# Trunk of one RG-LRU and one sparse-attention layer on one core: compressed-key scores as columns of the other score products, contiguous first loads

## The chip, the cores and the metric

The kernel runs on one core of one Trainium2 chip. Its time is device microseconds of one execution; three runs of the kernel before give a median of 574.55 us (574.05 to 574.77). The engines are named as in the profile: PE multiplies matrices (PEld loads its stationary operand), DVE and ACT work on rows of 128 partitions, POOL fills small tiles, SP issues most of the transfers. A "step" below is the distance from the start of one instruction to the start of the next on the same engine.

## The reference, cut to what matters

Two layers on x of 256 tokens by 1024 columns. Layer 0 is a recurrent block (two projections, a width-4 convolution, gates, a scan, an output projection), layer 1 is attention with three branches; a squared-ReLU MLP of 4096 follows each, with RMSNorm ahead of each part. The attention branches have their own keys and values and share the queries. With 256 tokens the selected and the window branch see all earlier keys. The compressed branch has 15 keys a group (padded to 16 in the kernel), and the change is about its scores:

```python
s_c = jnp.einsum('qghd,ngd->ghqn', qf, kc) - slopes * d_c.astype(jnp.float32)
p_c = _masked_softmax(s_c, d_c >= 0)
o_c = jnp.einsum('ghqn,ngd->qghd', p_c, vc)
...
s_s = jnp.einsum('qghd,gqkd->ghqk', qf, k_sel) - slopes * d_s[:, None].astype(jnp.float32)
...
s_w = jnp.einsum('qghd,kgd->ghqk', qf, kw) - slopes * d_w.astype(jnp.float32)
```

There are 16 heads in 4 groups of 4, 64 columns a head. Each score is the product of a query with a key, less a slope times the distance; a masked softmax follows for each branch.

## The kernel before

Activations lie transposed (128 columns of the model on the partitions, 256 tokens along the row). Every float32 product with weights is made of three products of float32r halves: a weight piece of 128 x 1024 lands in one of 5 raw buffers (`raw`, NRAW), ACT or DVE copies its high part to `whi` (L316, L268), DVE subtracts to get the low part `wlo` (L313, L277), and PE runs `mm3` (L308 to L310) for each of the 8 blocks of 128. A piece is 24 matmuls of 256 columns. There are 7 places for split pieces.

The two mixer layers are not written in program order: each step is given to a `Plan` with an engine, a cost, the keys that it reads and writes and a due time, and the plan (list scheduling, then passes backwards and forwards, with a seed) decides the order on each engine. HI tasks may go to ACT or DVE. The two MLPs are written out by hand.

**Start.** SP loads x in four parts of two chunks (L523 through `first_load`) and the first three weight pieces in halves (`raw0` keys), in the order of FIRST; the norm's gain for x comes as `vec[:, :8]`, a transfer of 32 bytes a partition that ACT issues (L532). `hh` is x times the gain on ACT (L558), `hl` the rest on DVE (L560). PE first runs WARM = 16 matmuls on a zero tile (L552), which feed nothing, then the first three pieces (the `c0`, `c1`, `c2` projections, in step with the chunks of x as they come).

**Gates.** In the recurrent layer, the square of the decay (`a2`) is a DVE multiplication, four of 128 x 512.

**Attention.** kh and kl hold the high and low part of the selected and the window keys, 512 columns a group; one half of the partitions of `sa` / `sb` holds the high part of a head's query and the other the low part, so that two matmuls (L1089 on kh, L1090 on kl) make the scores. For each head (`scores`) there are two such pairs: the first 128 queries against 2 x 128 keys, the other 128 queries against 2 x 256 keys. Each product goes to one of three PSUM banks in turn, and DVE adds the distances, writes the row and its extreme in one operation (L1096, a custom instruction and a read of its accumulator); ACT takes exponentials (L1099), DVE or ACT rescale (L1118, L1119), PE transposes (L1129) and multiplies with the values (L1144, `pv`). Between these the plan puts projections of queries and of the output as fillers. The compressed scores come from `compressed(a, ...)`, once for each four heads: eight matmuls of 32 columns (L1033; 16 high and 16 low columns of `kc`), then on DVE two additions from PSUM (L1043, L1044), a maximum (L1045), a subtraction (L1046), a product with the slopes (L1048), an exponential on ACT, a mask (L1050), a sum (L1051), the gate and the reciprocal (L1052, L1054), a product (L1055), then a transpose on PE (L1067) and a copy to `pc`, which `pv` reads first.

Of the kernel before, what the change touches and what calls it, by code (L numbers as in the profile page):

```python
# [19 lines left out]
P = 128  # L20
# [20 lines left out]
FIRST = "x0+ 00+ 10+ x2+ 20+ x4+ 02+ 12+ x6+ 22+ piece vec cst piece"  # L41
LAGS = (0.2, 0.25, 0.15, 0.13)

V_GM, V_GF, V_GL = 0, 16, 32
V_CW, V_CB, V_BA, V_BX, V_LAM = 40, 72, 80, 88, 96
V_PEK, V_PEV, V_BG = 104, 120, 136
V_N = 184
C_ID, C_D0, C_D1, C_DC, C_MC, C_BM, C_QS, C_SL = 0, 128, 256, 512, 544, 576, 584, 592
C_N = 608
# [170 lines left out]
def trunk_kernel(ctx: ExitStack, tc: tile.TileContext, x_in, vec_in, const_in, w2_in, wts, out):  # L220
# [40 lines left out]
    def split_hi(eng=None):  # L261
# [6 lines left out]
        (act.copy if eng is None else eng.tensor_copy)(hi_t[i % NSPL][:, :n], raw_t[i % NRAW][:, :n])  # L268
        state["split"] += 1

    def split_lo(eng=None):
# [5 lines left out]
        (eng or dve).tensor_tensor(lo[:, :n], raw_t[i % NRAW][:, :n], hi[:, :n].bitcast(F32), op=OP.subtract)  # L277
# [45 lines left out]
    class Section:  # L323


        def __init__(self):
# [3 lines left out]
            self.seen, self.join = dict(state), 1  # L330
            self.zs = {}

        def load(self, i, t):
            while self.seen["dma"] <= min(i, len(order) - 1):
                j = self.seen["dma"]
                self.seen["dma"] += 1
                self.add("sp", 1.5, lambda e, j=j: load(j), w=[("raw", j % NRAW), "loads"], t=t - 20 + j * 1e-3, lag=2.0)

        def split(self, i, t, lead):
# [3 lines left out]
            hi, lo, rw = hi_t[i % NSPL], lo_t[i % NSPL], raw_t[i % NRAW]  # L343
            if i >= self.seen["split"]:
                self.add([("act", 0.95, 0.0), ("dve", 0.63, HPEN)], copy(hi[:, :n], rw[:, :n]), r=[("raw", i % NRAW)],
                         w=[("hi", i % NSPL)], t=t)
                self.seen["split"] = i + 1
            if i >= self.seen["lo"]:
                self.add("dve", 1.14, diff(lo[:, :n], rw[:, :n], hi[:, :n]),
                         r=[("raw", i % NRAW), ("hi", i % NSPL)], w=[("lo", i % NSPL)], t=t)  # L350
# [104 lines left out]
    xt = xpool.tile([P, KC, S], F32, name="xt")  # L455
# [3 lines left out]
    consts.tile([P, 64], F32, name="edge")  # L459
# [53 lines left out]
    with ExitStack() as ph:  # L513
        rg = ph.enter_context(tc.tile_pool(name="rg", bufs=1))
        sec = Section()
        add, table = sec.add, sec.table
# [5 lines left out]
        def first_load(q, o, i, key, d):  # L522
            add(q, d, lambda e: (nc.scalar if e is act else nc.sync).dma_start(o, i), w=key + ["loads"] * (q == "sp"), t=-29.0, lag=1.9)  # L523

        def first_x(k, n=2):
            first_load("sp", xt[:, k:k + n], x_in[:, k:k + n], [("xt", k + i) for i in range(n)], (0.47, 0.73)[n - 1])

        def first_w(i, q, n=2):
            w = wts[offs[i]:offs[i + 1]].rearrange("(p n) -> p n", p=P)[:, q * 256:(q + n) * 256]
            first_load("sp", raw_t[i][:, q * 256:(q + n) * 256], w, [("raw0", i, q + j) for j in range(n)], (0.47, 0.73)[n - 1])  # L530
        sec.plan.busy["pool"] = 0.9
        nc.scalar.dma_start(vec[:, :8], vec_in[:, :8])  # L532
        add("sp", 0.0, lambda e: None, w=["vec0"], t=-31, lag=2.2)
        sec.seen.update(dma=NFINE, split=NFINE, lo=NFINE)
        for x in FIRST.split():
            n = 1 + x.endswith("+")
            if x == "piece":
                sec.load(sec.seen["dma"], -6)
            elif x == "cst":
                first_load("sp", cst, const_in, ["cst"], 1.0)  # L540
            elif x == "vec":
                first_load("sp", vec[:, 8:], vec_in[:, 8:], ["vec"], 0.47)
            elif x[0] == "x":
                first_x(int(x[1]), n)
            else:
                first_w(int(x[0]), int(x[1]), n)
# [4 lines left out]
        for i in range(WARM):  # L551
            pe.matmul(wz, warm[:, :P], warm, start=True, stop=True)  # L552

        x2 = rg.tile([P, KC, S], F32, name="x2")
        for k in range(KC):
            g = vec[:, V_GM + k:V_GM + k + 1]
# [24 lines left out]
        nc.gpsimd.dma_start(w2raw, w2_in)  # L581
# [797 lines left out]
```

## Time and profile before

| | us |
|---|---|
| median of three runs | 574.55 |
| the profiled execution, its own time | 573.78 |
| span of the profiled execution, first to last instruction | 572.0 |
| PE busy, DVE busy, ACT busy | 562.4, 410.3, 339.5 |
| recurrent layer on PE, about | 6 to 94 |
| first MLP on PE, about | 94 to 270 |
| attention layer on PE, about | 270 to 396 |
| second MLP and end, about | 396 to 572 |

The page gives busy time for each engine; a matmul is counted busy from its start to a modelled end, and matmuls overlap, so that a busy PE says only that it had no long gap. Whether PE lost time is read from the steps between the starts of its matmuls: where work flows, a 256-column matmul starts every 0.113 us, while each is shown as 0.28 us long.

### The profile page before, as it was taken

To read this page: it belongs to the slowest core of one execution; us is meant where nothing else is said; L and a number is where in the kernel's file an instruction comes from. 1 tells how busy PE (TensorE), PEld (TensorE's weight loads), DVE (VectorE), ACT (ScalarE), POOL (GpSimd) and SP (SyncE) were. 2 spreads that over 40 slices of the span, in tenths; PEclk is the share of its full clock that TensorE was granted. 3 is DMA by queue.
4 is the path that set the end of the run, shared out by engine and by line. 5 is a ranking of instruction groups with operands and counts; after the bars stand their busy time and mean duration, and the time that the engine had idled before them with its cause. 6 is when DMAs were issued, how large, how long until landed. Compare 5 with 4: busy or idle time off the path is not lost.

```text
span 572.0 us, 12346 instructions
## 1 busy us (share of the span) xinstructions
PE 562.4 (98%) x4896; PEld 553.3 (97%) x4896; DVE 410.3 (72%) x832; ACT 339.5 (59%) x663; POOL 44.9 (8%) x57
## 2 busy tenths in 40 slices
PE   7999999999999999999999999999999999999995
PEld 7999999999999999999999999899999999999995
DVE  6999999776775564565849999989866775563532
ACT  7699585866564443444557988866865564443410
POOL 2210000000000211221000000000000000222310
PEclk9999999999999999999999999999999999999998
DMA  8934576665667456556685132343676666467302
GB/s 290 395 122 148 171 241 197 211 208 189 190 197 241 150 196 223 170 190 227 213 268 170 35 111 64 141 148 111 215 228 186 190 200 237 150 201 223 129 1 73
DMA packets 32745, 103.66 MB, mean 181 GB/s; under 512 B 4000, under 2 KB 7584, under 8 KB 32688
## 3 DMA queue, kind: packets, MB, share of 16 engines
q1 hardware_dynamic: 31968, 102.36, 55.2%
q8 instruction: 38, 0.62, 0.5%
q10 hardware_dynamic: 688, 0.46, 0.2%
q14 instruction: 19, 0.16, 0.1%
q0 software_dynamic: 32, 0.07, 0.0%
HBM read 99.23 MB, written 1.05 MB: 175 GB/s over the span
## 4 chain that ended last, share of the span: by engine, by line
PE 97%; DVE 1%; DMA 1%; ACT 0%; issue 0%; DVEq 0%
PE bank L310 28%; PE bank L308 28%; PE bank L309 28%; PE bank L1144 3%; PE bank L667 2%; PE bank L1129 2%; PE bank L1089 1%; PE bank L1090 1%; PE bank L981 1%; DMA vec<-in_dram 1%; PE bank L982 1%; PE bank L983 1%; PE bank L931 1%; PE bank L1033 1%; DVE xg L1264 0%; DVE wlo L313 0%
## 5 line engine op out<-in xcount | busy, mean ns | idle before, releaser
L308 PE MATMUL bank<-hhl,whi 128*128 128x256 f32 x768 | 213.4, 278 | 1.3 <-DVE whi L316 1.3
L310 PE MATMUL bank<-hhl,wlo 128*128 128x256 f32 x768 | 212.5, 277 | 0.6 <-DVE wlo L313 0.6
L309 PE MATMUL bank<-hhl,whi 128*128 128x256 f32 x768 | 212.3, 276 | 0.0
L308 PEld LDWEIGHTS bank<-hhl,whi 128*128 128x128 f32 x768 | 144.2, 188 | 1.8 <-ACT whi L316 1.5
L310 PEld LDWEIGHTS bank<-hhl,wlo 128*128 128x128 f32 x768 | 144.2, 188 | 1.0 <-DVE wlo L313 1.0
L277 DVE TENSOR_TENSOR wlo<-raw,whi 128x1024 fp32r<-128x1024 f32 x115 | 143.2, 1266 | 1.9 <-ACT whi L268 1.9
L309 PEld LDWEIGHTS bank<-hhl,whi 128*128 128x128 f32 x768 | 144.2, 188 | 0.2
L308 PE MATMUL bank<-uhl,whi 128*128 128x256 f32 x512 | 141.5, 276 | 0.0
L309 PE MATMUL bank<-uhl,whi 128*128 128x256 f32 x512 | 141.4, 276 | 0.0
L310 PE MATMUL bank<-uhl,wlo 128*128 128x256 f32 x512 | 141.4, 276 | 0.0
L268 ACT CAST whi<-raw 128x1024 fp32r<-128x1024 f32 x116 | 118.1, 1039 | 23.1 <-issue 18.8
L308 PEld LDWEIGHTS bank<-uhl,whi 128*128 128x128 f32 x512 | 96.1, 188 | 0.0
L310 PEld LDWEIGHTS bank<-uhl,wlo 128*128 128x128 f32 x512 | 96.1, 188 | 0.0
L309 PEld LDWEIGHTS bank<-uhl,whi 128*128 128x128 f32 x512 | 96.1, 188 | 0.0
L313 DVE TENSOR_TENSOR wlo<-raw,whi 128x1024 fp32r<-128x1024 f32 (+2 forms) x74 | 79.2, 1093 | 7.8 <-ACT whi L316 7.7
L316 ACT CAST whi<-raw 128x1024 fp32r<-128x1024 f32 (+2 forms) x64 | 61.3, 966 | 18.8 <-DMA raw<-in_dram 5.3
L510 DVE TENSOR_TENSOR xt<-xt,bank 128x256 f32<-128x256 f32 x39 | 15.7, 418 | 74.3 <-PE bank L310 74.2
L764 ACT ACTIVATE u<-t 128x256 f32<-128x256 f32 x64 | 26.7, 417 | 58.1 <-DVE t L759 58.1
L759 DVE SCALAR_TENSOR_TENSOR t<-bank,rstd 128x256 f32<-128x256 f32 x64 | 26.9, 423 | 39.6 <-PE bank L310 39.6
L1099 ACT ACTIVATE pt<-pt,mx 128x128 f32<-128x128 f32 (+1 forms) x64 | 28.6, 450 | 2.9 <-DVE mx L1096 2.7
L480 POOL TENSOR_TENSOR acc<-xt 128x256 f32<-128x256 f32 x2 | 2.9, 1466 | 341.3 <-DVE xt L510 186.7
L766 DVE TENSOR_TENSOR uhl<-u,uhl 128x256 fp32r<-128x256 f32 x64 | 26.7, 416 | 3.0 <-ACT uhl L765 3.0
(207 smaller groups left out, 725.8 us busy)
## 6 DMA issues: line engine op xcount, KB each, us to landing
raw<-in_dram SPq DMA_DIRECT2D x173, 512.0 KB, 4.3
raw<-in_dram SPq DMA_DIRECT2D x4, 560.0 KB, 4.3
gw<-in_dram SPq DMA_DIRECT2D x4, 512.0 KB, 8.1
raw<-in_dram SPq DMA_DIRECT2D x6, 256.0 KB, 5.1
xt<-in_dram SPq DMA_DIRECT2D x4, 256.0 KB, 5.0
pT<-in_dram SPq DMA_DIRECT2D x2, 512.0 KB, 5.9
kh<-kh SPq DMA_DIRECT2D x8, 64.0 KB, 3.2
kl<-tl SPq DMA_DIRECT2D x8, 64.0 KB, 2.9
```

The lines of the kernel that those rows point to most:

```text
L268: (act.copy if eng is None else eng.tensor_copy)(hi_t[i % NSPL][:, :n], raw_t[i % NRAW][:, :n])
L277: (eng or dve).tensor_tensor(lo[:, :n], raw_t[i % NRAW][:, :n], hi[:, :n].bitcast(F32), op=OP.subtract)
L308: pe.matmul(ps, wh, xh, start=start, stop=False)
L309: pe.matmul(ps, wh, xl, start=False, stop=False)
L310: pe.matmul(ps, wl, xh, start=False, stop=stop)
L313: return lambda e: e.tensor_tensor(o, a, h.bitcast(F32), op=OP.subtract)
L316: return lambda e: (e.copy if e is act else e.tensor_copy)(o, a)
L759: dve.scalar_tensor_tensor(t, z, 0.0, rs, op0=OP.max, op1=OP.mult)
L764: act.activation(u, t, AF.Square)
L766: later(lambda: dve.tensor_tensor(ul[m], u, uh[m].bitcast(F32), op=OP.subtract))
L1099: add("act", (0.39, 0.49)[qc], lambda e, row=row, j=j: e.activation(row, row, AF.Exp, bias=mx[:, j:j + 1], scale=-1.0, accum_out=sm[:, j:j ...
L1144: two = lambda c, w, y, **k: [e.matmul(o()[own_(hf), c0 + c.start:c0 + c.stop], w(hf), y(hf), **k) for hf in range(2)]
```

## The change

- The compressed keys move into kh and kl: a group has now 528 columns (first 128 selected keys, 16 compressed keys, the other 128 selected keys, 256 window keys). `kc`, its clearing on POOL and the eight 32-column matmuls of `compressed` are gone.
- A head's scores are three pairs instead of two: 288 columns for the first 128 queries (128 selected + 16 compressed, 128 window + 16 that nobody reads), 272 for the other queries' selected and compressed keys, 256 for their window keys. Each pair takes one of the same three banks.
- For each head, two DVE operations of 128 x 16 with the accumulator (L1116 of the new kernel) take the compressed scores out of the banks, with distance and slope; `compressed` keeps its steps from the subtraction on, without the slopes' product. Its due times move from 0.5, 4, 8.5, 12 to 3.5, 7.5, 11.5, 15.2 (in units of a head's 5 us), after the heads that feed it.
- x, the gain and the halves of the first three pieces lie in DRAM so that each first transfer reads one contiguous block; the gain comes as 8 more columns of the first x transfer (520 columns) and ACT's transfer is gone. The constants are 592 columns instead of 608. The load of `w2raw` moves from POOL's queue to SP's.
- Two more places for weight pieces: pieces 5 and 6 land in halves of `y`, which is written later.
- WARM is 18, and 8 more matmuls on the zero tile stand after the first six real ones. The square `a2` is on ACT. Planned costs, lags and the first section's seed differ, and so does the order of that section.

```diff
-CST = (0.5, 4.0, 8.5, 12.0)
-SEEDS, ROUNDS, SHIFT = (3, 5), 6, 1.5
+CST = (3.5, 7.5, 11.5, 15.2)
+SEEDS, ROUNDS, SHIFT = (64, 5), 6, 1.5
-WARM = 16
+WARM = 18
...
+    spare = [None, None]
+    def raw_of(i):
+        n = NRAW + len(spare)
+        return raw_t[i % NRAW if i < NRAW else (i - n) % NRAW] if i < NRAW or i >= n else spare[i - NRAW]
...
-        nc.scalar.dma_start(vec[:, :8], vec_in[:, :8])
-        add("sp", 0.0, lambda e: None, w=["vec0"], t=-31, lag=2.2)
+        def first_x(k):
+            a, b = KC * (k > 0) + k * S, KC + (k + 2) * S
+            src = x_in[P * a:P * b].rearrange("(p n) -> p n", p=P)
+            first_load(xgt[:, a:b], src, [("xt", k), ("xt", k + 1)] + ["vec0"] * (k == 0), 0.66, 3.6 if k else 2.0)
+        def first_w(i, q):
+            o = offs[i] + P * q * 256
+            src = wts[o:o + P * 512].rearrange("(p n) -> p n", p=P)
+            first_load(raw_t[i][:, q * 256:q * 256 + 512], src, [("raw0", i, q), ("raw0", i, q + 1)], 0.66, 3.6 if q or i else 2.1)
...
-        nc.gpsimd.dma_start(w2raw, w2_in)
+        add("sp", 0.35, lambda e: e.dma_start(w2raw, w2_in), w=["loads"], t=30.0)
+        spare[:] = [y_b[:, 4 * i:4 * i + 4].rearrange("p k s -> p (k s)") for i in range(2)]
...
+                        if m == 0 and k == 1:
+                            keep_warm(8)
...
-            add("dve", 0.6, lambda e: e.tensor_tensor(a2, rp, rp, op=OP.mult), r=keys("r", m), w=[ak], t=t + 2)
+            add("act", 0.53, lambda e: e.activation(a2, rp, AF.Square), r=keys("r", m), w=[ak], t=t + 2)
...
-            add("pe", 0.76, run, r=xk + ["kch", ("kcl", 0), ("kcl", 1)], w=b7, t=t)
-                (0.2, lambda e: e.tensor_tensor(s, sc()[:, :, :, 0], dc, op=OP.add), b7, [sk]),
-                (0.2, lambda e: e.tensor_tensor(s, sc()[:, :, :, 1], s, op=OP.add), b7, [sk]),
-                (0.2, lambda e: e.tensor_reduce(mx, f2, axis=AX.X, op=OP.max), [sk], [mk]),
-                (0.2, lambda e: e.tensor_tensor(f3, f3, sl, op=OP.mult), [], [sk]),
...
+            parts = ((0, lambda x: cview(x, PC, PC), lambda y: kpair(y, g, PC), (0, 1), 0.26),
+                     (1, lambda x: x[:, :S + NCP], lambda y: y[:, g * GK:g * GK + S + NCP], (0,), 0.25),
+                     (1, lambda x: x[:, :S], lambda y: y[:, g * GK + S + NCP:(g + 1) * GK], (1,), 0.23))
...
+                    e.matmul(view(z()), x[:, qs], keys_(kh), start=True, stop=False)
+                    e.matmul(view(z()), x[:, qs], keys_(kl), start=False, stop=True)
...
+                if 0 in sets:
+                    add("dve", 0.22, lambda e, z=z, qc=qc: e.tensor_tensor_reduce(
+                        css[a % 2][:, cj, qc], z()[:, P:PC], cst[:, C_DC + qc * NCP:C_DC + (qc + 1) * NCP], -slope, -NEG, OP.add,
+                        OP.min, cmx[a % 2][:, 2 * cj + qc:2 * cj + qc + 1]),
+                        r=bk + ["cst", ("sq", 0), ("sq", 1)], w=[("cs", a % 2), ("cm", a % 2)], t=t + 0.35)
```

Three places in the order of the instructions follow. The first is PE at the start, after the first three real matmuls (`bank_188` and, in the new kernel, `bank_186` belong to piece 0, `bank_200` and `bank_209` to piece 1). Before:

```order
L308 MATMUL bank_188<-hhl,whi_83 128x256
L309 MATMUL bank_188<-hhl,whi_83 128x256
L310 MATMUL bank_188<-hhl,wlo_90 128x256
L308 MATMUL bank_200<-hhl,whi_84 128x256
L309 MATMUL bank_200<-hhl,whi_84 128x256
L310 MATMUL bank_200<-hhl,wlo_91 128x256
```

After:

```order
L318 MATMUL bank_186<-hhl,whi_83 128x256
L319 MATMUL bank_186<-hhl,whi_83 128x256
L320 MATMUL bank_186<-hhl,wlo_90 128x256
L567 MATMUL bank_122<-warm 128x256 x8
L318 MATMUL bank_209<-hhl,whi_84 128x256
L319 MATMUL bank_209<-hhl,whi_84 128x256
L320 MATMUL bank_209<-hhl,wlo_91 128x256
```

Eight matmuls on the zero tile now stand between piece 0's first two chunks and piece 1's.

The second is PE in the attention layer at the second head, `sa` and `sb` being the queries of even and odd groups. Before, with the compressed scores of the first four heads ahead of it:

```order
L1033 MATMUL bank_3785<-kc,sa_3216 128x32 x2
L1033 MATMUL bank_3785<-kc,sb_3220 128x32 x2
L1033 MATMUL bank_3785<-kc,sa_3217 128x32 x2
L1033 MATMUL bank_3785<-kc,sb_3221 128x32 x2
L1089 MATMUL bank_3800<-kh,sb_3220 128x512
L1090 MATMUL bank_3800<-kl,sb_3220 128x512
```

After:

```order
L1098 MATMUL bank_3794<-kh,sb_3229 128x256
L1099 MATMUL bank_3794<-kl,sb_3229 128x256
L1098 MATMUL bank_3799<-kh,sb_3229 128x288
L1099 MATMUL bank_3799<-kl,sb_3229 128x288
L1098 MATMUL bank_3804<-kh,sb_3229 128x272
L1099 MATMUL bank_3804<-kl,sb_3229 128x272
```

The 32-column matmuls are gone and the head fills three banks with 272 and 288 columns where it had 512 and 256.

The third is PE near the end of the attention layer, at the product with the values of the heads 12 and 13 (`pc` is the transposed compressed softmax). Before, it follows the scores of the last head:

```order
L1089 MATMUL bank_4717<-kh,sb_3223 128x512
L1090 MATMUL bank_4717<-kl,sb_3223 128x512
L1144 MATMUL bank_4722<-pc_3244,bd 64x128 x4
L1144 MATMUL bank_4722<-pT,vv 64x256 x2
L1144 MATMUL bank_4722<-pT,vv 64x128 x2
```

After, it follows the compressed transpose and the last head's transposes:

```order
L1072 MATMUL bank_4818<-cst,sq_112 128x128
L1147 MATMUL bank_4820<-cst,pt 128x128 x3
L1147 MATMUL bank_4824<-cst,pt 128x128 x3
L1162 MATMUL bank_4831<-pc_3252,bd 64x128 x4
L1162 MATMUL bank_4831<-pT,vv 64x256 x2
```

The last compressed softmax now stands behind all scores, and both last value products behind it; ahead of it, after the last scores, stand 36 filler matmuls and one head's six transposes.

## Rows read from the trace of the kernel before

**Rows 1.** The page: busy time of each engine, and the chain that ended last by engine.

```profile
PE 562.4 (98%) x4896; PEld 553.3 (97%) x4896; DVE 410.3 (72%) x832; ACT 339.5 (59%) x663; POOL 44.9 (8%) x57
...
PE 97%; DVE 1%; DMA 1%; ACT 0%; issue 0%; DVEq 0%
```

**Rows 2.** Windows of the recurrent layer and of the first MLP: stretch, its length, then busy time and count of PE, PEld, DVE, ACT, POOL, the granted clock, DMA share and GB/s.

```profile
10.00:20.00 10.00, 10.00 (x90) 10.00 (x89) 9.57 (x21) 7.71 (x16) 4.04 (x2) 1.00 0.95 361
...
40.00:60.00 20.00, 20.00 (x158) 19.46 (x158) 20.00 (x32) 19.86 (x33) 0.00 (x0) 1.00 0.41 129
...
100.00:150.00 50.00, 50.00 (x443) 50.00 (x443) 36.30 (x62) 33.52 (x64) 0.00 (x0) 1.00 0.64 202
```

**Rows 3.** The timeline of all engines from 0 to 9 us: start, duration, engine, line, operation, count, and the idle time ahead of it with what ended it.

```profile
0.74 0.41 ACTq L532 DMA_DIRECT2D vec<-in_dram  x1
...
1.28 3.78 PE L552 MATMUL bank<-warm 128*128 128x256 f32 x16 [1.28 <-POOL warm L549]
...
4.96 0.91 ACT L558 ACTIVATE hhl<-xt,vec 128x256 fp32r<-128x256 f32 x2 [2.28 <-DMA vec<-in_dram]
...
5.50 0.48 DVE L560 SCALAR_TENSOR_TENSOR hhl<-xt,vec,hhl 128x256 fp32r<-128x256 f32 x1 [4.62 <-ACT hhl L558]
...
5.90 0.29 DVE L316 CAST whi<-raw 128x256 fp32r<-128x256 f32 x1
...
6.33 0.36 PE L308 MATMUL bank<-hhl,whi 128*128 128x256 f32 x1 [1.26 <-DVE whi L316]
...
6.97 0.39 PE L310 MATMUL bank<-hhl,wlo 128*128 128x256 f32 x1 [0.16 <-DVE wlo L313]
```

**Rows 4.** PE's timeline after that; from 6.33 to 10.00 it lists 20 steps.

```profile
9.19 0.39 PE L310 MATMUL bank<-hhl,wlo 128*128 128x256 f32 x1 [0.42 <-DVE wlo L313]
...
10.00 0.28 PE L310 MATMUL bank<-hhl,wlo 128*128 128x256 f32 x1
```

**Rows 5.** DMA issues from 0.7 to 1.15 us and, last row, from 1.1 to 1.5 us (the first half of weight piece 0, issued at 1.18): count, size of each, us from issue to landing.

```profile
xt<-in_dram SPq DMA_DIRECT2D x1, 256.0 KB, 4.0
vec<-in_dram ACTq DMA_DIRECT2D x1, 4.0 KB, 4.2
...
raw<-in_dram SPq DMA_DIRECT2D x1, 256.0 KB, 4.2
```

**Rows 6.** Half-microsecond windows at the start, columns as in rows 2; the last two are DMA share and GB/s.

```profile
2.50:3.00 0.50, 0.50 (x5) 0.50 (x4) 0.00 (x0) 0.18 (x1) 0.00 (x0) 1.00 0.75 121
...
4.50:5.00 0.50, 0.50 (x3) 0.27 (x2) 0.00 (x0) 0.04 (x1) 0.00 (x0) 1.00 1.02 393
```

**Rows 7.** PE's timeline in the attention layer: the first head's scores and a half of the second's, then the first compressed block.

```profile
305.52 0.39 PE L1089 MATMUL bank<-kh,sa 128*128 128x512 f32 x1
305.75 0.39 PE L1090 MATMUL bank<-kl,sa 128*128 128x512 f32 x1
305.98 0.28 PE L1089 MATMUL bank<-kh,sa 128*128 128x256 f32 x1
...
306.21 0.28 PE L1089 MATMUL bank<-kh,sb 128*128 128x256 f32 x1
...
307.80 0.29 PE L1033 MATMUL bank<-kc,sa 128*128 128x32 f32 x2
...
308.61 0.48 PE L1089 MATMUL bank<-kh,sb 128*128 128x512 f32 x1
308.92 0.40 PE L1090 MATMUL bank<-kl,sb 128*128 128x512 f32 x1
```

**Rows 8.** The same at the last of the four compressed blocks.

```profile
354.85 0.29 PE L1033 MATMUL bank<-kc,sa 128*128 128x32 f32 x2
...
355.65 0.36 PE L308 MATMUL bank<-oh,whi 128*128 128x256 f32 x1
355.86 0.28 PE L309 MATMUL bank<-ol,whi 128*128 128x256 f32 x1
```

**Rows 9.** DVE's timeline in the attention layer: two score operations with the reads of their accumulator, then two steps of the compressed softmax with a small operation between.

```profile
306.44 0.41 DVE L1096 CUSTOM_DVE_ANT_0 pt<-bank,cst 128x256 f32<-128x256 f32 x1
306.78 0.08 DVE L1096 DVE_READ_ACCUMULATOR2_ANT mx<- 128x1 f32 x1
306.78 0.29 DVE L1096 CUSTOM_DVE_ANT_0 pt<-bank,cst 128x128 f32<-128x128 f32 x1
306.99 0.08 DVE L1096 DVE_READ_ACCUMULATOR2_ANT mx<- 128x1 f32 x1
...
309.64 0.15 DVE L1109 SCALAR_TENSOR_TENSOR sm<-sm,gts 128x4 f32<-128x4 f32 x1
309.76 0.29 DVE L1044 TENSOR_TENSOR sq<-bank,sq 128x128 f32<-128x128 f32 x1
309.97 0.17 DVE L1111 RECIPROCAL sm<-sm 128x4 f32<-128x4 f32 x1
```

**Rows 10.** The sum of four windows from 305 to 385 us, the attention stretch with scores: busy time of each engine out of 80 us.

```profile
sum 80.00, PE 80.00 PEld 74.35 DVE 75.13 ACT 65.60 POOL 0.00; mean PE 20.00 PEld 18.59 DVE 18.78 ACT 16.40 POOL 0.00
```

**Rows 11.** PE's timeline at the last head: its first scores, and its transposes.

```profile
369.79 0.28 PE L1089 MATMUL bank<-kh,sb 128*128 128x256 f32 x1
...
376.36 0.82 PE L1129 MATMUL bank<-cst,pt 128*128 128x128 f32 x6
```

**Rows 12.** DVE's timeline there: the last head's rescaling.

```profile
373.33 0.74 DVE L1119 TENSOR_SCALAR pt<-pt,sm 128x128 f32<-128x128 f32 x3
```

More of the change, by code (lines that the diff above doesn't have):

```diff
@@ L336, in load @@
                 self.seen["dma"] += 1
-                self.add("sp", 1.5, lambda e, j=j: load(j), w=[("raw", j % NRAW), "loads"], t=t - 20 + j * 1e-3, lag=2.0)
+                self.add("sp", self.dma[0], lambda e, j=j: load(j), w=[raw_key(j), "loads"], t=t - 20 + j * 1e-3, lag=self.dma[1])
         def split(self, i, t, lead):
@@ L520, in trunk_kernel, with first_load @@
         table(AF.Sqrt, -30)
[L522 to L531, printed above, removed]
-        nc.scalar.dma_start(vec[:, :8], vec_in[:, :8])
-        add("sp", 0.0, lambda e: None, w=["vec0"], t=-31, lag=2.2)
+        def first_load(o, i, key, d, lag=3.6):
+            add("sp", d, lambda e: e.dma_start(o, i), w=key + ["loads"], t=-29.0, lag=lag)
+        def first_x(k):
[6 more added lines that the diff above has]
+            first_load(raw_t[i][:, q * 256:q * 256 + 512], src, [("raw0", i, q), ("raw0", i, q + 1)], 0.66, 3.6 if q or i else 2.1)
+        sec.plan.busy.update(pool=0.5, act=0.4, pe=4.4)
         sec.seen.update(dma=NFINE, split=NFINE, lo=NFINE)
         for x in FIRST.split():
-            n = 1 + x.endswith("+")
             if x == "piece":
@@ L550, in trunk_kernel, with keep_warm @@
         wz = bank(7)[:, :S]
-        for i in range(WARM):
-            pe.matmul(wz, warm[:, :P], warm, start=True, stop=True)
+        def keep_warm(n):
+            for i in range(n):
+                pe.matmul(wz, warm[:, :P], warm, start=True, stop=True)
+        keep_warm(WARM)
         x2 = rg.tile([P, KC, S], F32, name="x2")
         for k in range(KC):
-            g = vec[:, V_GM + k:V_GM + k + 1]
+            g = gm0[:, k:k + 1]
             t = 0.6 * k - 3
@@ L1083, in scores, with run @@
                 bk = [("ps", b)]
[L1084 to L1086 removed]
+                z = zview(("s", s, i), b, lambda x: x)
+                def run(e, z=z, qc=qc, view=view, keys_=keys_):
                     qs = slice(qc * P, (qc + 1) * P)
[L1088 to L1092 removed]
+                    e.matmul(view(z()), x[:, qs], keys_(kh), start=True, stop=False)
+                    e.matmul(view(z()), x[:, qs], keys_(kl), start=False, stop=True)
+                add("pe", d, run, r=xk + ["kl", "kch", ("kcl", 0), ("kcl", 1)] + kkeys(g, 0) + kkeys(g, 1), w=bk, t=t)
+                for b in sets:
                     o, j = qc * 2 * P + b * nk, 2 * qc + b
@@ L1280, in _arrange @@
     x = f["x"][0]
-    xT = np.ascontiguousarray(x.reshape(S, KC, P).transpose(2, 1, 0))
     cols = lambda v: v.reshape(-1, P).T
+    xT = np.concatenate([cols(f["norm_mix"][0]), x.reshape(S, KC, P).transpose(2, 1, 0).reshape(P, -1)], axis=1)
+    ends = [0] + [KC + k * S for k in (2, 4, 6, 8)]
+    xT = np.concatenate([xT[:, a:b].reshape(-1) for a, b in zip(ends, ends[1:])])
     dup = lambda a: np.concatenate([a, a], axis=0)
```

125 lines of the change are left out of this document (60 added, 65 removed).

## The prediction

> **What bounds the kernel now.** I read the page's busy line and chain first [rows 1]: PE is busy 98% of the span and is 97% of the chain that ended last; no other engine is over 72%. Since matmuls overlap, this alone could hide stalls, so the windows come next [rows 2]. From 100 to 150 us 443 matmuls start in 50 us, one each 0.113 us; from 10 to 20 us it is 90, 0.111. So PE flows from 10 us on. In the gates' stretch, 40 to 60 us, DVE is busy 20.0 and ACT 19.9 of 20 us and PE still has no idle time. What is left to gain is PE's own work, and the time until its flow begins.
>
> At the start [rows 3, 4] PE runs 16 matmuls on the zero tile from 1.28, is idle for 1.26, begins at 6.33, and takes until 10.00 for 20 steps. At 0.1133 these are 2.27 us, so 1.40 of the 3.67 are waits for operands. As if PE had begun at 6.33 + 1.40 = 7.73 and never waited.
>
> In the attention layer PE is busy without a break, and DVE is busy 75.13 of 80 us [rows 10]: 4.87 us of slack on DVE, 14.4 on ACT. These two bounds lie close together, so DVE has to be counted too.
>
> **The change part by part.**
>
> *Compressed blocks removed.* The eight matmuls of 32 columns start at 307.80 and the next pair at 308.61, 0.81 us; that pair's first step is 0.31 where a 512-column one is 0.23 [rows 7], so 0.08 more goes with the block. At the last block it is 0.80 + 0.09 [rows 8]. Four blocks of 0.89: **-3.56**. A matmul of 32 columns costs 0.10, hardly less than one of 256 (0.115): it brings its own stationary operand. The Trainium skill ("TensorE: Matmul & The Clock Gate", Wait — 56ns, not 53.3ns?) gives a floor of about 25 ns from start to start for matmuls of 32 columns; by it the blocks would hold only 32 x 0.025 = 0.8 us and the sum below would be -0.3 instead of -3.0. The rows show four times that, and the measurement decides.
>
> *Columns added.* A head takes 2 x 0.23 + 2 x 0.115 = 0.69 now [rows 7]. By 0.23 / 512 = 0.45 ns a column, 288, 272 and 256 columns take 0.130, 0.1225 and 0.115, twice each 0.735. 16 x 0.045 = **+0.72**. One more pair a head brings 16 more starts that wait for a bank. Such a start costs nothing at 305.52 and 0.08 to 0.09 at 308.61 and 355.65 [rows 7, 8]: 0 to 1.4. I take **+0.5**, since most starts have another pair ahead of them, as the one at 305.98 does, at no cost.
>
> *DVE in the attention layer.* 32 operations of 128 x 16 with an accumulator are new. No row has one. A score operation of 256 columns has a step of 0.34, one of 128 a step of 0.21; the read of the accumulator starts with the next operation and adds nothing [rows 9]. That is 1.0 ns a column, and 0.10 for 16 columns; the 128 x 4 row's step is 0.12. The bounds are 0.10 and 0.21, and the small row is nearest: 32 x 0.10 = 3.2, at most 6.7. Gone are 16 steps of 0.21 (two additions, a maximum, a product for each four heads): 3.4. The new order also moves work: counted in the two orders, DVE loses three casts of weight pieces net (0.6 each) and gains four of queries (0.2 each), and ACT the reverse. DVE's sum falls by about 1, or rises by 2.3 at the upper bound, within its 4.87 us of slack less the 2.3 by which PE's stretch shrinks. ACT's sum rises by about 2 of its 14.4. I take **0**; if that cover is gone, PE waits for the excess.
>
> *The later compressed softmax.* The last compressed softmax now waits for the last head's scores, and both last value products wait for it. Now the last head's scores start at 369.79 and its rescaling ends at 374.07, 4.3 us [rows 11, 12]; its transposes come at 376.36. The compressed chain is shorter than four score rows and their rescaling: seven small DVE steps of 0.1 to 0.3, one exponential, a transpose and a copy, some 3 us. In the new order 36 fillers (4.1 us), six transposes (0.6) and the scores themselves (0.74) cover it, 5.4 in all. Cost **0**; without this cover up to 1.
>
> *Start.* The gain's transfer of 4 KB lands 4.2 after 0.74, at 4.94, and ACT begins at 4.96, having waited 2.28 for it; x's first part landed at 4.74, piece 0's first half at 1.18 + 4.2 = 5.38 [rows 3, 5]. Removing that wait alone lets ACT begin 0.2 earlier. From 2.5 to 3 us the DMA engines are 75% busy but move 121 GB/s, against 393 at 4.5 to 5 [rows 6]: contiguous blocks could bring the first data up to 1.3 us earlier (0.5 MB at 393 GB/s is 1.3 us, and the transfers begin at about 2). PE can't begin before its 18 zero matmuls end, 1.28 + 18 x 0.236 = 5.5. The eight inside the first pieces cost 8 x 0.113 = 0.9 unless PE would have waited there. Best: 5.5 + 0.9 = 6.4 against 7.73, a gain of 1.3. Worst inside this case: the data land as before; ACT 0.2 earlier, DVE's cast no longer behind the first `hl`, so PE begins near 6.1, waits 0.3 for the first `wlo`, loses 0.9 to the zero matmuls, and later waits of 0.4 stay: as if from 7.7, no gain. I take the middle, **-0.7**.
>
> *The rest, at nothing.* Two more raw places let transfers run ahead, but PE waits for none after 10 us [rows 2]. `a2` on ACT is four operations of 0.5 to 0.6 where ACT has no idle time; the cover is PE's run of branch projections behind the gates, 192 matmuls or 21.8 us, and if it failed PE would wait up to 2. The shorter constants, `w2raw` on SP (one more issue among loads that run ahead; read in the attention layer) and the fill of kl on POOL lie beside other work.
>
> *Sum.* -3.56 + 0.72 + 0.5 - 0.7 = **-3.0**. The profiled execution took 573.78, so 570.7 by its own time; it lies 0.77 below the median, 574.55. Against the median I predict **571.5**.
>
> **The rivals.**
>
> *A. PE doesn't get the time in the attention layer (no measurable change).* Three pairs over three banks make each head wait until DVE has emptied a bank: 16 heads by 0.2, the step of one score operation [rows 9], is 3.2 back, and with the rest of the sum 574.7. By the rule of the Trainium skill named above the blocks would hold 0.8 instead of 3.56, which gives 574.2. Against it: DVE follows a pair within 0.2 to 0.7 [rows 7, 9].
>
> *B. DVE becomes the bound in the attention layer (slower).* If the 128 x 16 operations run apart from their accumulator reads at the full lengths of the 128-column row, 0.29 + 0.08 = 0.37 [rows 9], they take 11.8; less 3.4 removed it is 8.4 more, against 4.87 of slack [rows 10]. PE's stretch then grows by 3.6 instead of falling by 2.3; with the start's 0.7 the kernel takes 577.4. It turns slower by over 0.2% when an operation costs over (4.87 + 3.4 + 0.7 + 1.15) / 32 = 0.32. Against it: each read starts with the next operation.
>
> *C. The start gives more, or takes.* If the first data come 1.3 earlier and the zero matmuls fill waits, 570.9. On the zero tile a matmul takes 3.78 / 16 = 0.236 us [rows 3], twice the later 0.113, that is the lower of the two clock levels (1.2 and 2.4 GHz), though the granted clock stands as 1.00 there [rows 6]; by 7 us the steps are short. If real work begins before the clock has risen, the first six and the eight zero matmuls cost 14 x 0.12 = 1.7 more, and the start loses 0.4 to 1: 573.0. For it: PE would begin earlier. Against it: two more zero matmuls stand ahead.
>
> **How the numbers follow.** Forecast, with both forms of C: 0.83. A: 0.12. B: 0.05. The ends: all bank starts free, the best start, and 0.5 of waits in the attention layer gone as DVE's sum falls gives -3.56 + 0.72 - 1.3 - 0.5 = -4.6, 569.9. At the other end all starts at 0.09 (+1.4) and no gain at the start give -1.4, 573.1; the slow clock of C lies there too. I set the range at 569.8 to 573.4, with A and B outside it. About 0.2%, 1.15 us, is what a measurement of this kernel can tell from no change. Faster than 573.4: 0.83. Within 0.2%: 0.13, A and B short of its point. Slower: 0.04, B beyond its point.
>
> **What would show it.** In the profile after: no 32-column matmuls; pairs of 288, 272 and 256 columns with steps near 0.130, 0.1225, 0.115, and few of 0.2 or more at their first (a bank wait, A); the 128 x 16 operations with steps near 0.10 (0.3 would be B); DVE's idle time over the attention stretch above 2 us; no gap at PE before the last two value products. From the first fillers to the end of the attention layer PE should need 2.3 us less. At the start: ACT's first `hh` without a wait for the gain, PE's first real matmul between 5.5 and 6.1, and step sums to 20 us that put the flow 0 to 1.3 earlier. The prediction is wrong in its mechanism if the attention layer doesn't shorten, and in its size if the start moves by more than 1.3 either way.

## The result and the profile after

The changed kernel takes **570.9 us** (median of six runs, 570.45 to 571.77) where the kernel before takes 574.51 (six runs beside it, 574.05 to 574.86). The ratio is 0.9934, 95% interval 0.9924 to 0.9945. The profiled execution took 571.1, with a span of 569.3. That is only 2.68 below the profiled execution of before, since that one lay 0.73 below its own median and this one 0.20 above; so single stages are compared over all executions profiled here, and the total by medians.

The page of the changed kernel, answering to [rows 1]:

```profile
PE 560.9 (99%) x4906; PEld 553.7 (97%) x4906; DVE 407.0 (71%) x877; ACT 342.7 (60%) x666; POOL 40.1 (7%) x55
...
PE 95%; DVE 2%; issue 1%; DMA 1%; ACT 1%; DVEq 0%; POOL 0%; SPq 0%; ACTq 0%; POOLq 0%
```

PE still sets the time, as before. So I cut the span where PE starts something recognizable, and take the differences of these start times from PE's timeline:

| stretch of PE | before | after | difference |
|---|---|---|---|
| span's start to first matmul of the first down projection | 175.54 | 174.32 | -1.22 |
| from there to the first matmul of the attention layer | 87.17 | 87.17 | 0 |
| attention layer's first matmul to the first score matmul | 42.81 | 43.96 | **+1.15** |
| first score matmul to the second down projection | 170.17 | 167.66 | -2.51 |
| second down projection, first to last matmul | 87.77 | 87.77 | 0 |

Two stretches are as forecast in sign and near in size. The third should not have moved.

**The start.** All engines' timeline of the changed kernel, 0 to 9 us, and one row of PE at 10, answering to [rows 3]:

```profile
1.28 4.21 PE L567 MATMUL bank<-warm 128*128 128x256 f32 x18 [1.28 <-POOL warm L562]
...
3.44 0.91 ACT L574 ACTIVATE hhl<-xt 128x256 fp32r<-128x256 f32 x2 [1.21 <-DMA xt<-in_dram]
...
5.28 0.39 PE L318 MATMUL bank<-hhl,whi 128*128 128x256 f32 x1
...
6.09 1.11 PE L567 MATMUL bank<-warm 128*128 128x256 f32 x8
...
10.06 0.28 PE L320 MATMUL bank<-hhl,wlo 128*128 128x256 f32 x1
```

Its first DMA issue, and the half microsecond from 2.5, answering to [rows 5, 6]:

```profile
xt<-in_dram SPq DMA_DIRECT2D x1, 260.0 KB, 2.7
```

```profile
2.50:3.00 0.50, 0.50 (x4) 0.50 (x4) 0.00 (x0) 0.00 (x0) 0.00 (x0) 1.00 1.01 323
```

x's first part lands 2.7 after its issue in place of 4.0 (3.5 in e2, e6 and e12 below, which have the old start), the DMA engines move 323 GB/s in place of 121, ACT begins 1.5 earlier, and PE goes from its zero matmuls to real work without a gap. PE's first real matmul, at 5.28, is earlier than the 5.5 to 6.1 that I named as a sign: the zero matmuls start 0.21 apart (0.38 once), not 0.236, since I had divided a length that includes the modelled end of the last one. The 30th real matmul starts at 10.06, as if PE had begun at 10.06 - 29 x 0.1133 = 6.77 and never waited; before, the same sum gave 7.73.

**The scores.** PE's timeline at the first head of the changed kernel, answering to [rows 7]; then DVE's at the same head, answering to [rows 9]:

```profile
305.45 0.29 PE L1098 MATMUL bank<-kh,sa 128*128 128x272 f32 x1
305.57 0.29 PE L1099 MATMUL bank<-kl,sa 128*128 128x272 f32 x1
305.70 0.30 PE L1098 MATMUL bank<-kh,sa 128*128 128x288 f32 x1
305.84 0.30 PE L1099 MATMUL bank<-kl,sa 128*128 128x288 f32 x1
305.97 0.28 PE L1098 MATMUL bank<-kh,sa 128*128 128x256 f32 x1
306.09 0.28 PE L1099 MATMUL bank<-kl,sa 128*128 128x256 f32 x1
```

```profile
306.39 0.17 DVE L1116 CUSTOM_DVE_ANT_0 sq<-bank,cst 128x16 f32<-128x16 f32 x1
306.48 0.08 DVE L1116 DVE_READ_ACCUMULATOR2_ANT cm<- 128x1 f32 x1
306.48 0.28 DVE L1109 CUSTOM_DVE_ANT_0 pt<-bank,cst 128x128 f32<-128x128 f32 x1
```

The pairs take 0.13, 0.13 and 0.12 a matmul, and no 32-column matmul is left. A new 128x16 operation takes a step of 0.09: its accumulator is read beside the next operation.

**What was not foreseen.** At the matmuls over the compressed inputs, 64 by count, PE now waits. PE's timeline after, then before:

```profile
278.85 0.41 PE L955 MATMUL bank<-pt,pT 128*64 128x62 f32 x2
279.62 3.61 PE L955 MATMUL bank<-pt,pT 128*64 128x62 f32 x62 [0.36 <-DMA pt<-tt]
285.34 0.43 PE L965 MATMUL bank<-sq,w2raw 64*128 64x64 f32 x2 [0.36 <-ACT sq L959]
```

```profile
280.07 3.69 PE L931 MATMUL bank<-pt,pT 128*64 128x62 f32 x64
```

After two of them PE stands until moves into pt land, and the next product (of `sq`) waits once more. The moves come late because DVE's read of the fourth projected input waits for its buffer (one of three, `tt`) until a move out of it has landed. DVE's row after, then before:

```profile
276.47 0.42 DVE L938 TENSOR_TENSOR tt<-bank,rstd 128x256 f32<-128x256 f32 x1 [3.02 <-DMA pt<-tt]
```

```profile
277.05 0.42 DVE L914 TENSOR_TENSOR tt<-bank,rstd 128x256 f32<-128x256 f32 x1 [1.59 <-DMA pt<-tt]
```

From the layer's first matmul (261.49 and 262.71) that is 14.98 in place of 14.34. The first six moves are issued as early as before (9.46 to 12.59 behind the layer's first matmul, before 9.47 to 12.58), but they take 4.1 from issue to landing in the median, before 3.5.

### The profile page after: what moved, and what is told of

The parts are those of the page before. It is cut to its first block, busy times and chain, and to the rows that moved or that the text cites. A ratio compares the mean times of both kernels' runs of the same rounds, so it can differ in the third digit from the quotient of the medians.

```text
span 569.3 us, 12420 instructions
## 1 busy us (share of the span) xinstructions
PE 560.9 (99%) x4906; PEld 553.7 (97%) x4906; DVE 407.0 (71%) x877; ACT 342.7 (60%) x666; POOL 40.1 (7%) x55
## 4 chain that ended last, share of the span: by engine, by line
PE 95%; DVE 2%; issue 1%; DMA 1%; ACT 1%; DVEq 0%; POOL 0%; SPq 0%; ACTq 0%; POOLq 0%
PE bank L318 28%; PE bank L319 27%; PE bank L320 27%; PE bank L1162 3%; PE bank L686 2%; PE bank L1147 2%; PE bank L1098 1%; PE bank L1099 1%; PE bank L567 1%; DMA pt<-tt 1%; PE bank L1005 1%; DVE wlo L323 1%; PE bank L1006 1%; PE bank L1007 1%; ACT whi L326 1%
## 5 line engine op out<-in xcount | busy, mean ns | idle before, releaser
L323 DVE TENSOR_TENSOR wlo<-raw,whi 128x1024 fp32r<-128x1024 f32 (+2 forms) x72 | 77.4, 1091 | 7.0 <-ACT whi L326 6.9
L326 ACT CAST whi<-raw 128x1024 fp32r<-128x1024 f32 (+2 forms) x63 | 60.0, 966 | 21.4 <-PE bank L319 9.1
L1112 ACT ACTIVATE pt<-pt,mx 128x256 f32<-128x256 f32 (+1 forms) x64 | 28.7, 450 | 3.6 <-DVE mx L1109 3.2
L498 ACT ACTIVATE hhl<-xt,vec 128x256 fp32r<-128x256 f32 x8 | 4.1, 510 | 39.4 <-DVE xt L522 39.4
```

Of the source, the lines that this page charges most:

```text
L323: return lambda e: e.tensor_tensor(o, a, h.bitcast(F32), op=OP.subtract)
L326: return lambda e: (e.copy if e is act else e.tensor_copy)(o, a)
L1112: add("act", (0.39, 0.49)[qc], lambda e, row=row, j=j: e.activation(row, row, AF.Exp, bias=mx[:, j:j + 1], scale=-1.0, accum_out=sm[:, j:j ...
```

## The experiments

Each run stands beside the kernel before, whose median was 574.37 beside e1 to e4, 574.54 beside e5 to e8 and 574.58 beside e9 to e12; a median here is that of 4 (e10) to 11 (e12) executions:

| run | median us | ratio to before, 95% |
|---|---|---|
| e1, start only | 572.97 | 0.9973 (0.9962 to 0.9984) |
| e2, attention only | 572.40 | 0.9969 (0.9958 to 0.9981) |
| e3, no inner zero matmuls | 570.71 | 0.9941 (0.9929 to 0.9954) |
| e4, fourth buffer | 569.60 | 0.9917 (0.9903 to 0.9930) |
| e5, small operations twice | 572.34 | 0.9960 (0.9947 to 0.9974) |
| e6, blocks twice in before | 577.98 | 1.0059 (1.0045 to 1.0072) |
| e7, strided first loads | 570.83 | 0.9935 (0.9924 to 0.9946) |
| e8, ten zero matmuls | 572.18 | 0.9959 (0.9948 to 0.9971) |
| e9, gain apart | 570.78 | 0.9937 (0.9924 to 0.9949) |
| e10, e3 and e4 together | 569.11 | 0.9904 (0.9889 to 0.9919) |
| e11, no small operations | 570.55 | 0.9926 (0.9914 to 0.9938) |
| e12, fourth buffer in before | 573.78 | 0.9989 (0.9980 to 0.9998) |

**e1 and e2, the two halves.** All edits of one half at a time; the line that stands for each:

```diff
 # e1: the changed kernel
-CST = (3.5, 7.5, 11.5, 15.2)
+CST = (0.5, 4.0, 8.5, 12.0)
...
-                e.matmul(view(z()), x[:, qs], keys_(kh), start=True, stop=False)
+                e.matmul(sp_(), x[:, qs], krow(kh), start=True, stop=False)
 # e2: the kernel of before, the same lines the other way
```

> The changed kernel with the attention layer of before (compressed blocks of 32 columns, its own times and order); start, first loads, raw places and recurrent layer stay changed. My theory: the edits add up, and the start keeps the 1.2 us by which the first down projection came earlier in the changed kernel's trace (174.32 against 175.54): 574.5 - 1.2 = 573.3. Rival: what the start gains is lost again before the end, 574.5. For the 1.2 us that the changed kernel lost at the matmuls over the compressed inputs: if the attention layer's new order costs it, the time from that layer's first matmul to the first 304-column value matmul is 20.98 here as in before; if the new start or chance costs it, it is near 21.67 as in the changed kernel.

> The kernel of before with only the attention layer of the changed kernel (compressed keys as columns, three pairs a head); start and recurrent layer as before. My theory: 2.5 us come from the scores: 574.5 - 2.5 = 572.0, or 573.2 if the loss of 1.2 at the compressed inputs belongs to the new order (21.67 from the layer's first matmul to the first 304-column value matmul), and the score stretch from the first score matmul to the second down projection is 167.7 against 170.2. Rival: the scores gain only together with the new start, through transfers that run ahead: 574.5 and a score stretch near 170.

e1 gains 1.40 and e2 1.97 (574.37 less each median), 3.37 together against 3.6 for the whole: the edits add up. The score stretch is 170.07 in e1 and 167.81 in e2, so the 2.5 belong to the attention layer's edits and need nothing of the start's. The stretch ahead of them goes with the attention layer's order: 42.70 in e1, 43.55 in e2. Over all profiled executions with the layer's own three buffers it is 42.70 to 43.00 in the old order (before, e1, e6) and 43.06 to 43.96 in the new (after, e2, e3, e5, e7, e8, e9, e11; mean 43.54). So the new order costs 0.7 there on average, and varies more.

**e4 and e12, the buffer.** The fourth projected input goes to a tile not in use yet; the order of work is the same.

```diff
-            return tt[n % 3], ("tt", n % 3), tl[n % NTL], ("tl", n % NTL)
+            return bd.rearrange("p a b c -> p (a b c)")[:, :S] if n == 4 else tt[n % 3], ("tt", n % 3), tl[n % NTL], ("tl", n % NTL)
```

> The changed kernel, with the fourth projected compressed input written to free room (the tile bd, not in use yet) instead of the first of three tt buffers, in the same order of work. My theory: the fourth projection's read on DVE waits 3.0 us until a move out of that buffer lands, so the last two moves are issued late, PE waits 0.66 for them and 0.42 behind them; without the wait the moves land before PE asks: 570.9 - 1.1 = 569.8, and the time from the layer's first matmul to the first 304-column value matmul falls from 21.67 to about 20.9. Rival: the moves are late because the transfers of the weights hold the queues, and come no earlier than now: 570.9.

> The kernel of before with the same free room for the fourth projected compressed input. In its order PE doesn't wait for the moves, and DVE's wait of 1.6 us for the buffer stands beside PE's run of key projections. My theory: the buffer cost the changed kernel time only by its new order, and here at most the 0.2 us that PE waits behind the first hidden product comes back: 574.4. Rival: the buffer held back both orders alike, 573.2.

DVE's and PE's timelines of e4:

```profile
273.99 0.42 DVE L938 TENSOR_TENSOR bd<-bank,rstd 128x256 f32<-128x256 f32 x1
```

```profile
279.32 3.69 PE L955 MATMUL bank<-pt,pT 128*64 128x62 f32 x64
284.67 0.32 PE L965 MATMUL bank<-sq,w2raw 64*128 64x64 f32 x1
```

Neither DVE nor PE waits any more, and the stretch is 42.41 (42.40 in e10): 1.1 below the mean of the new order. The time falls by 1.3 (570.9 to 569.6). In the order of before the same edit brings the stretch to 42.42, 0.4 less, and the time to 573.78: the interval of its ratio ends just under 1. With the fourth buffer both orders need the same 42.4. So the buffer is the cause, and the new order made it dearer; e12's forecast of 0.2 at most was low. A part of that is chance: the first six moves take 3.2 to 4.1 in the executions of the new order with the old buffers, and the stretch follows them, from 43.06 (e5, 3.2) to 43.96 (after, 4.1); the old order has 3.3 to 3.7. At equal landing the new order still costs 0.5 to 0.6 more: 43.31 (e7) and 43.55 (e2) at 3.5 and 3.7, against 42.81 (before) and 42.99 (e6). What in the order does that was not separated.

**e6, the price of a 32-column matmul.**

```diff
-                        e.matmul(sc()[:, j, qc].rearrange("p i n -> p (i n)"), xq, kc[:, g].rearrange("p i n -> p (i n)"),
-                                 start=True, stop=True)
+                        for _ in range(2):
+                            e.matmul(sc()[:, j, qc].rearrange("p i n -> p (i n)"), xq, kc[:, g].rearrange("p i n -> p (i n)"),
+                                     start=True, stop=True)
```

> The kernel of before with each of the 32 matmuls of 32 columns issued twice in a row (the second writes the same result again). My theory: each costs 0.10 of PE, since it brings its own stationary operand: 32 x 0.103 = 3.3, 574.4 + 3.3 = 577.7, the score stretch grows from 170.2 to 173.5. Rival, the floor of 25 ns from start to start for 32 columns that the Trainium skill states (TensorE: Matmul & The Clock Gate, Wait — 56ns, not 53.3ns?): 32 x 0.025 = 0.8, 575.2.

PE's timeline at e6's first block:

```profile
308.56 0.51 PE L1034 MATMUL bank<-kc,sa 128*128 128x32 f32 x4
308.92 0.60 PE L1034 MATMUL bank<-kc,sb 128*128 128x32 f32 x4
309.37 0.60 PE L1034 MATMUL bank<-kc,sa 128*128 128x32 f32 x4
309.81 0.60 PE L1034 MATMUL bank<-kc,sb 128*128 128x32 f32 x4
310.26 0.48 PE L1090 MATMUL bank<-kh,sb 128*128 128x512 f32 x1
```

The first of its rows of weight loads (PEld):

```profile
308.44 0.53 PEld L1034 LDWEIGHTS bank<-kc,sa 128*128 128x128 f32 x4
```

Sixteen take 1.70, 0.106 each; each of them loads its own stationary operand, the repeated ones too (four loads to four matmuls in every row). The median rises by 3.44 and the score stretch by 3.6. The floor of about 25 ns for 32 columns in the Trainium skill ("TensorE: Matmul & The Clock Gate", Wait — 56ns, not 53.3ns?) would have given 0.8; it doesn't hold for matmuls that each load a 128 x 128 stationary operand. The same page (Back-to-back issue gap) says that in a stream of such pairs both operations set the spacing, with 81 ns for 128 columns; the rows here agree in kind.

**e5 and e11, DVE's slack.**

```diff
 # e5
-                    add("dve", 0.22, lambda e, z=z, qc=qc: e.tensor_tensor_reduce(
+                    add("dve", 0.22, lambda e, z=z, qc=qc: [e.tensor_tensor_reduce(
...
-                        OP.min, cmx[a % 2][:, 2 * cj + qc:2 * cj + qc + 1]),
+                        OP.min, cmx[a % 2][:, 2 * cj + qc:2 * cj + qc + 1]) for _ in range(2)],
 # e11: in its place
+                    add("dve", 0.22, lambda e, qc=qc: cj == qc == 0 and [e.memset(y[a % 2], 0.0) for y in (css, cmx)],
```

> The changed kernel with each of the 32 new 128x16 operations on DVE issued twice, in the same order of work. In the trace of the changed kernel such an operation takes a step of 0.09, so 32 x 0.09 = 2.9 us go to DVE, which is idle for 5.4 of the 80 us from 305 to 385. My theory (term of 0, covered by DVE's slack): no change, 570.9, the score stretch stays at 167.7. Rival, DVE as the second bound: the slack lies where it can't be used, and half to all of the 2.9 shows, 572.4 to 573.8.

> The changed kernel without the 32 new 128x16 operations on DVE (the compressed scores are left out: zeros stand in their place, written by eight fills), PE's work and all orders as they are. DVE loses 2.9 us and gets 1.1 at most of fills. If DVE binds in part, as the run with these operations twice suggests (half of 2.9 showed), 0.9 comes back: 570.0. If DVE's slack hid them, 570.9.

Busy time from the first score matmul to the last product with the values, for before, after, e5 and e11, columns as in [rows 2]:

```profile
305.52:380.58 75.06, 75.06 (x684) 69.58 (x682) 71.72 (x304) 63.27 (x203) 0.00 (x0) 1.00 0.34 99
```

```profile
305.45:377.94 72.49, 72.47 (x684) 68.68 (x682) 68.39 (x350) 64.06 (x202) 0.00 (x0) 1.00 0.31 94
```

```profile
304.88:378.97 74.09, 73.49 (x684) 68.87 (x682) 72.03 (x414) 64.22 (x202) 0.00 (x0) 1.00 0.29 91
```

```profile
304.19:376.68 72.49, 72.47 (x683) 68.69 (x682) 66.55 (x294) 63.93 (x202) 0.00 (x0) 1.00 0.31 92
```

The fixed windows of [rows 10] and of my expectations also take in work behind the scores; here each row holds the same work. DVE is idle for 4.1 of 72.5 us in the changed kernel, 3.3 of 75.1 before. e11 takes 1.8 off DVE and e5 adds 3.6, 0.11 for each repeated operation.

With 1.8 less on DVE the score stretch stays as it was (167.64 against 167.66); the time, 570.55, is not told apart from 570.9. With 3.6 more it grows by 1.55 (169.21), and PE shows it. PE's timeline at one place in the changed kernel, then in e5, then e5's DVE:

```profile
337.73 0.82 PE L1147 MATMUL bank<-cst,pt 128*128 128x128 f32 x6
338.30 0.37 PE L1098 MATMUL bank<-kh,sb 128*128 128x272 f32 x1
338.51 0.29 PE L1099 MATMUL bank<-kl,sb 128*128 128x272 f32 x1
```

```profile
337.89 0.82 PE L1147 MATMUL bank<-cst,pt 128*128 128x128 f32 x6
339.26 0.36 PE L1098 MATMUL bank<-kh,sb 128*128 128x272 f32 x1 [0.55 <-DVE cm L1059]
```

```profile
338.69 0.42 DVE L1109 CUSTOM_DVE_ANT_0 pt<-bank,cst 128x256 f32<-128x256 f32 x1
```

From the transposes to the next scores 1.37 pass in e5 and 0.57 in the changed kernel. PE waits for DVE, by all appearance for a score bank that DVE has not emptied: its read of a bank (L1109) ends at 339.11, and L1059, which PE's row names, is the small operation right behind it. So my theory held for the change as made (e11) and failed for the same load once more (e5): DVE's idle time hides the new operations, and of 3.6 more only a part.

**e7, e9, e3, e8: the start.**

```diff
 # e7: x, likewise the weight pieces, from rows as long as before
-            src = x_in[P * a:P * b].rearrange("(p n) -> p n", p=P)
+            src = x_in[:, a:b]
 # e9
+            if k == 0:
+                nc.scalar.dma_start(gm0, src[:, :KC])
+                a, src = KC, src[:, KC:]
 # e3
-                            keep_warm(8)
+                            keep_warm(0)
 # e8
-WARM = 18
+WARM = 10
```

> The changed kernel with its first loads (x and the first three weight pieces) from the layout of before, in which a partition's part lies in a longer row, with the same sizes, order and gain inside x. My theory: the contiguous blocks bring the first data earlier; without them ACT's first product begins near 4.6 in place of 3.44, PE's flow starts near 7.5 in place of 6.8, and the time is 571.6. Rival: only the wait for the gain's own transfer was lost before, and ACT begins near 3.4 here too: 570.9.

> The changed kernel with the gain (8 numbers a partition) fetched by a transfer of its own from ACT, as before, and x's first part without it; all else as changed. My theory after the strided run: the gain's own transfer is what held the start; ACT's first product begins at 4.4 to 5.0 again in place of 3.4 to 3.9, the first real matmul comes near 5.9 in place of 5.28, and the time is 571.5. Rival: the 18 zero matmuls hold PE until 5.28 and the clock's rise comes at 5.5 to 7.7 anyway, so nothing is lost: 570.9.

> The changed kernel without the eight zero matmuls inside the first weight pieces. My theory, the cover that I named: PE would have waited there for operands anyway, so the first real flow stays where it is: 570.9, with waits for the second part of x in place of the zero matmuls. Rival 1: they hold PE for their 0.9 us: 570.0. Rival 2: without them the idle time brings the slow matmuls of 0.236 us back (14 or more at 0.12 extra): 572 or more.

> The changed kernel with 10 zero matmuls at the start in place of 18. The operands of the first real matmul are there at about 4.6, 0.7 before the 18 zero matmuls end. My theory: PE begins at 4.6, but its flow then waits for the second part of x, which ACT has at 6.6 to 7.0 in all runs: no change, 570.9. Rival 1: the 0.7 stays gained, 570.2. Rival 2: the matmuls of twice the length last until about 7 whatever is fed, and more of the real work falls among them: 571.5 or more.

ACT's and PE's rows of e7, then ACT's of e9:

```profile
3.87 0.91 ACT L573 ACTIVATE hhl<-xt 128x256 fp32r<-128x256 f32 x2 [1.65 <-DMA xt<-in_dram]
...
5.28 0.43 PE L318 MATMUL bank<-hhl,whi 128*128 128x256 f32 x1
```

```profile
3.90 0.91 ACT L577 ACTIVATE hhl<-xt 128x256 fp32r<-128x256 f32 x2 [1.22 <-DMA xt<-in_dram]
```

Strided loads put ACT 0.43 later, a gain of its own 0.46. Neither reaches PE, which leaves its zero matmuls at 5.28 in both, and neither moves the time (570.83 and 570.78). My theories of e7 and e9 fall, the rivals hold. Where both stood together, with the start of before, ACT began at 4.40 to 4.46 in e2, e6 and e12 (4.96 in the profile of before) and PE 1.37 to 1.38 later, at 5.78 to 5.83 (6.33): the two delays together would be longer than the 18 zero matmuls. That is argued; both together with 18 zero matmuls were not tried. Nor was the new order of this section tried by itself. In all four executions with the old start (before, e2, e6, e12) one step of PE takes 0.71, from 8.48 to 9.19 in before, and ends with DVE's low part of the weights (the first of [rows 4]); with the changed start and 18 zero matmuls no step between 2 and 10 us is longer than 0.4. So the order may hold up to 0.6 of the start's gain. PE's row in before, ahead of the first of [rows 4]:

```profile
8.48 0.28 PE L309 MATMUL bank<-hhl,whi 128*128 128x256 f32 x1
```

e8's PE timeline:

```profile
1.28 2.50 PE L567 MATMUL bank<-warm 128*128 128x256 f32 x10 [1.28 <-POOL warm L562]
4.73 0.58 PE L318 MATMUL bank<-hhl,whi 128*128 128x256 f32 x1 [0.95 <-ACT whi L326]
...
9.30 0.41 PE L318 MATMUL bank<-hhl,whi 128*128 128x256 f32 x1
9.51 0.33 PE L319 MATMUL bank<-hhl,whi 128*128 128x256 f32 x1
9.68 0.28 PE L320 MATMUL bank<-hhl,wlo 128*128 128x256 f32 x1
```

With ten zero matmuls PE starts real work 0.55 earlier and then runs at 0.21 a matmul or slower until 9.5; rival 2 holds, at +1.3. So the zero matmuls do more than fill the wait for the loads: with eight fewer, PE stands idle for 0.95 and its steps stay long for 2 to 5 us more than with 18. For e3 nothing can be told by the median, 0.2 lower; its flow to 10 us is as if from 6.33, its 33rd real matmul starting at 9.96. That is 0.44 ahead of the changed kernel, as is its first down projection (173.88 against 174.32), and inside the spread of the runs that have the eight (below). So they may cost half of their 0.9, or nothing.

**e10, the two edits together.**

> The changed kernel with the fourth buffer for the compressed inputs and without the eight zero matmuls inside the first pieces: the two edits of earlier runs together. If both add up, 569.6 - 0.2 = 569.4; if the zero matmuls are worth their 0.9 us when the clock has risen, 568.7; if they bring the clock up earlier, as the run with ten zero matmuls at the start hints, 569.6 or a little more.

569.11 is the lowest median here, between the first two forecasts. Its interval overlaps that of e4, so the fourth buffer is shown, and the eight inner zero matmuls are at best 0.5 worth leaving out. e10's own trace shows what stands behind the start. Its flow begins as if at 6.13, 0.6 ahead of the changed kernel, but PE then waits where the norm's statistics come in:

```profile
21.36 0.71 PE L519 MATMUL bank<-cst,rcol 128*128 128x128 f32 x4 [0.33 <-DVE rcol L414]
```

It reaches the first down projection at 174.57, no earlier than the changed kernel (174.32).

## Why the prediction was right, and where not

**Blocks removed, -3.56.** Right: the same 32 matmuls once more cost 3.44 (e6). In the trace of before their steps sum to 3.32.

**Columns and bank starts, +0.72 and +0.5.** The steps of all score matmuls sum to 12.21 before and 13.16 after, +0.95 in place of 1.22. The columns were sized well; the start term was too high, and its reason was wrong. Of the first matmuls of a pair 12 of 48 take 0.08 to 0.09 more, before 10 of 32. All 22 stand right behind transposes or a 32-column matmul, as at 338.30 above, and none behind other scores or projections; in the score stretch every matmul of 256 columns or more that comes right behind one of these has the same excess, projections too, 20 before and 18 after. The two rows that I priced such a start from, 308.61 and 355.65, stand right behind a compressed block, and the second is a projection. So no wait for a bank shows in these steps, and rival A fell with room to spare. The score stretch fell by 2.51, forecast 2.34.

**DVE in the attention layer, 0.** Right, and the step of 0.10 too (0.09 here); e11 shows the cover, e5 its end. DVE's busy time over the stretch fell by 3.3, forecast 1, and ACT's rose by 0.8, forecast 2. Rival B's price was far off, but its point is nearer than I put it: in e5 an operation costs 0.09 and 0.11 for its repetition, 0.20 in all, short of the 0.32 from which the kernel would turn slower, and the stretch already loses 1.55 of the 3.6 that e5 adds.

**The later softmax, 0.** Right: PE's transpose of the last compressed softmax takes a step of 0.11 (372.51 to 372.62). Behind it only the step ahead of the last value product is longer than usual, 0.30 in place of 0.21.

**The start, -0.7.** Size within its bounds, reason wrong. By the sum to 10 us the flow begins as if at 7.73, 7.78, 8.19 and 7.84 with the start of before (before, e2, e6, e12), and at 6.77, 6.64, 7.25, 7.12 and 6.32 with the changed one (after, e1, e4, e5, e11): 7.89 and 6.82 in the mean, -1.07. I put the gain on the contiguous blocks; taken back alone they change nothing (e7). The clock, which I had as a rival, is a part of the term (e8). What the rest of the gain comes from, of loads, gain, zero matmuls and order, stays open.

**The rest, at nothing.** Here the prediction failed twice. From the start of the flow, so reckoned, to the first down projection it was 167.8 to 167.9 in the four executions with the old start and is 167.5 to 167.6 in the five with the new one, -0.3; which edit brings it (`a2` on ACT, the raw places, the new order) was not separated. And I counted the new order's work only from 305 us on: the stage over the compressed inputs, moved by the same plan, lost 0.7. These two, the larger start and the smaller start term of the scores cancel in part: -1.07 - 0.3 + 0.7 - 2.51 = -3.2, forecast -3.0, measured -3.6 by the medians. That the sum of the stages comes within 0.2 of the forecast is luck in part, and 0.4 of the medians' difference has no stage that I could name (by its interval the ratio is worth 3.2 to 4.4 us).

## What to carry to other kernels

When a plan is made anew, read its order in every stage that it plans, the untouched ones too, and look there for reads that wait for a buffer until a transfer out of it has landed. Two delays beside each other at a start have to be priced together: either one alone cost nothing here, and both together may cost what sticks out (argued, not tried). An engine's idle time is cover only in part: 1.8 us less on DVE brought the score stretch nothing, 3.6 us more cost it 1.55, with 4.1 of 72.5 us idle. And look at what stands ahead of a slow step before naming its cause: the excess that I took for a wait for a bank came wherever transposes or short matmuls stood ahead.

## What the runs showed of the hardware

The time at which 256-column matmuls go from 0.21 apart (the lower level, 1.2 GHz) to 0.113 (2.4 GHz) differs between executions with the same program ahead of it: in the nine executions with 18 zero matmuls the first short step starts at 4.38 (e11) to 7.39 (e3 and e4). e10 and e3 are alike up to there: in e10 the 18 zero matmuls end early and the first real step is 0.12, in e3 the nine real matmuls from 5.28 to 6.99 still take 0.21. PE's timeline of e10, then of e3:

```profile
1.28 3.90 PE L567 MATMUL bank<-warm 128*128 128x256 f32 x18 [1.28 <-POOL warm L562]
5.02 0.28 PE L318 MATMUL bank<-hhl,whi 128*128 128x256 f32 x1
5.14 0.28 PE L319 MATMUL bank<-hhl,whi 128*128 128x256 f32 x1
```

```profile
6.99 0.41 PE L320 MATMUL bank<-hhl,wlo 128*128 128x256 f32 x1
7.20 0.35 PE L318 MATMUL bank<-hhl,whi 128*128 128x256 f32 x1
```

In both PE had run zero matmuls without a break from 1.28. The window from 5 to 7 us of either shows a granted clock of 1.00, so here the steps tell the level and that column doesn't. Windows of e3, then of e10:

```profile
5.00:7.00 2.00, 2.00 (x12) 2.00 (x11) 1.69 (x5) 1.50 (x6) 0.00 (x0) 1.00 0.99 349
```

```profile
5.00:7.00 2.00, 2.00 (x14) 1.56 (x13) 1.75 (x6) 1.69 (x6) 0.00 (x0) 1.00 1.04 336
```
